# Single K tiles in the first two splits of weights, another order of the first loads, and other slots for the pairs' steps of attention

## The chip, the core and the metric

The kernel runs on one core of one Trainium2 chip. The metric is the device time of that core in microseconds (us): the median of the runs of a program.

## What is computed

Two layers, each with one input projection, two branches of mixing, and one output projection; 256 positions, D = 2048, float32 throughout. Cut to what matters:

```python
def hybrid_layer(x, ...):
    h = rmsnorm(x, norm_g)
    c_a, c_glu, c_gate, q_down, kv_down, k_pe, m_gate, g_conv, g_mla = split(h @ w_in)
    # branch A: convolution
    u = c_a * sigmoid(c_glu)
    u = causal_depthwise_conv(u, conv_w, width=31) + conv_b
    y_conv = (silu(layernorm(u)) * silu(c_gate)) @ w_proj_conv
    # branch B: 16 heads, query and key of 192 (128 plain, 64 rotary), value of 128
    q = rmsnorm_per_head(rmsnorm(q_down) @ w_uq)            # then rope on 64 of 192
    k_nope, v = split(rmsnorm(kv_down) @ w_ukv)
    k = rmsnorm_per_head(concat(k_nope, k_pe))              # then rope on 64 of 192
    o = softmax(q @ k.T * 192**-0.5, mask: key chunk <= query chunk, chunks of 64) @ v
    y_mla = (o * silu(m_gate)) @ w_proj_mla
    y = sigmoid(g_conv) * y_conv + sigmoid(g_mla) * y_mla
    return x + y @ w_out
```

## The kernel before

**Products.** Every float32 product is made of three products of TensorE's F32R type. A matrix is split into `hi` (a cast to F32R) and `lo` (what the cast left); the three are hi·hi, hi·lo and lo·hi. Weights come as *pieces* of two K tiles (`KS` = 2; a K tile is 128 rows, by 512 columns, or 384 for `uq`) on SP's DMA queue (`load`, four pieces ahead). `split_hi` has ScalarE cast a piece three ahead, `split_lo` has VectorE subtract it two ahead, and `product` runs a *block* (a weight matrix by up to 512 columns): for each piece twelve matmuls, six for each half `t` of the positions, in the order that `order_of_products` gives. Only piece 0 is loaded and split by single K tiles. A block's accumulators are evacuated one slot after its last piece; blocks take turns on two sets of accumulators.

**The order of work.** `order_of_layer` writes it out: a `glu` block (8 pieces), the three `down` blocks, two more `glu`, and then for each of the 8 pairs of heads `uq` (2 pieces), `ukv` (2 pieces), and a `glu` or `cgate` block (8 pieces): a period of 12 pieces, about 35 us. Then the gates and the projections follow.

**Slots.** After each piece `background` counts a clock on by one and issues whatever is due: first the steps that `at_slot` entered for this slot or an earlier one, then, as far as a budget of VectorE's time lasts, the next entries of `fill` (the taps of the depthwise convolution, one by one), and, by a budget of ScalarE's, a tap scaled ahead (`assist`): VectorE then adds it with one instruction (an *added* tap) in place of two (*direct* taps). `InOrder` chains the instructions of each engine, so that an engine's order in the program is the order in which the steps were called. As it also issues them, every instruction in the profile stands at its line, L127.

**A pair's steps.** `attention(b)` enters them all once the pair's `ukv` block is issued, at slots counted from there: `stats` (norm factors of q and k), `scale_k` (scales k by its factor and parks q and k in DRAM through GpSimd's queue, `turn_d`), `back_in("qk")` (fetches them transposed in 32-blocks), `blockwise` (VectorE transposes within the blocks), `split_nope` and `split_rope` (casts on ScalarE, subtractions on VectorE one slot later), `scores` (TensorE, tile `s`), `maxima`, `exponentials` (ScalarE, tile `pr`, parked through GpSimd), `back_in("p")`, `turn_p` (transposes `pr`), `split_p` (casts and subtracts them into tile `pv`, which also holds the values), `values`, `outputs`. With a period of 12 slots and steps out to slot 34, the steps of three pairs are interleaved at any time.

**A glu block's end.** `glu_evac` has ScalarE compute the sigmoid and VectorE the product, both named `su` in the rows; the accumulators are free when VectorE has read them. The block after the next one, `ukv`, takes the same accumulators.

**The start.** ScalarE's queue loads the gains with x's first tile (`gx`), then x's tiles 1, 2–3 and 4–5; SP's loads pieces 0, 1, 2, then x's tiles 6–7, piece 3, x's 8–11, piece 4, x's 12–15. `first_h` scales a tile of x by its gain (`h_hi` on ScalarE, `h_lo` on VectorE); `split_hi` calls it ahead of the cast of the piece that needs it. `warm` is a chain of matmuls on zeros, ahead of the first product.

Of the kernel before, what the change touches and what calls it, by code (L numbers as in the profile page):

```python
# [12 lines left out]
F32 = mybir.dt.float32  # L13
F32R = mybir.dt.float32r
# [6 lines left out]
P = 128  # L21
T = 2
# [33 lines left out]
R_QA, R_KVA, R_QR, R_KR, R_N = 0, LORA, 2 * LORA, 2 * LORA + ROPE, 2 * LORA + 2 * ROPE  # L56

KS = 2
N_WARM = 8

# [1 line left out]
EVAC_AT = 1  # L64
FETCH_AT, TURNED_AT = 4, 8

STATS_AT, SCALE_AT, QK_BACK_AT, QK_TURN_AT, NOPE_AT, ROPE_AT, SCORES_AT = 2, 3, 6, 11, 12, 14, 17
MAX_AT, EXP_AT, P_BACK_AT, P_TURN_AT, P_SPLIT_AT, VALUES_AT, O_AT = 18, 19, 23, 28, 30, 32, 34

REVOLUTION_PIECES = 6  # L70

# [44 lines left out]
def trunk(ctx: ExitStack, tc: tile.TileContext, xT, x, g_in, pos, win, wuq, wukv, wpc, wpm, wo, cst, rows, invf, out):  # L116
# [19 lines left out]
    pe, vec, act, gps, sp = (InOrder(e) for e in (nc.tensor, nc.vector, nc.scalar, nc.gpsimd, nc.sync))  # L136
# [7 lines left out]
    work = pool("work", 1)  # L144
# [7 lines left out]
    tp_p = pool("tp", 2, space=PSUM)  # L152
# [30 lines left out]
    def load(i):  # L183
        if i >= len(pieces) or i in loaded:
            return
        ap, n = pieces[i]
        loaded[i] = t = raw_p.tile([P, KS, n], F32, tag="raw", name=f"raw{i}")
        for a in range(0, KS, 1 if i == 0 else KS):
            k = slice(a, a + 1 if i == 0 else KS)
            sp.dma_start(t[:, k, :], ap[:, k, :])  # L190

    def split_hi(i):
        if i >= len(pieces) or i in highs:
            return
        load(i)
        highs[i] = split_p.tile([P, KS, pieces[i][1]], F32R, tag="hi", name=f"hi{i}", bufs=4)
        for a in range(0, KS, 1 if i == 0 else KS):
            k = slice(a, a + 1 if i == 0 else KS)

            for step in ("w", "h") if i == a == 0 else ("h", "w"):  # L200
                if step == "w":
                    act.copy(highs[i][:, k], loaded[i][:, k])
                    if i == 0:
                        split_lo(0, k)
                elif i * KS < NCT:
                    for c in range(i * KS + k.start, i * KS + k.stop):
                        first_h(c)
        for a in range(1, LOAD_AHEAD + 1):
            load(i + a)

    def split_lo(i, k=slice(0, KS)):
        if i >= len(pieces) or done.get(i, (0, 0, 0))[2] >= k.stop:
            return
        lo = done[i][1] if i in done else split_p.tile([P, KS, pieces[i][1]], F32R, tag="lo", name=f"lo{i}")
        vec.tensor_sub(lo[:, k], loaded[i][:, k], highs[i][:, k].bitcast(F32))
        done[i] = highs[i], lo, k.stop
# [61 lines left out]
    def order_of_products(i, last):  # L278

        two = range(2)
        if i == 0:
            return [(t, kk, p) for kk in range(KS) for p in ((0, 1, 2) if kk else (0, 2, 1)) for t in range(T)]
        high, low = (lambda t, p: [(t, kk, p) for kk in range(KS)]), (lambda t: [(t, kk, 2) for kk in range(KS)])
        if last:
            return high(0, 0) + high(0, 1) + high(1, 0) + low(0) + high(1, 1) + low(1)
        return [e for t in two for p in two for e in high(t, p)] + low(0) + low(1)

    def product(planned, stat, evacuate, evac_at=EVAC_AT, costs=(0.0, 0.0), before=None):  # L290
        nk, n, mine = planned
        blocks_begun[0] += 1
        pts = [acc_p.tile([P, 512], F32, tag=f"acc{blocks_begun[0] % 2}{t}", name=f"acc{mine[0]}_{t}") for t in range(T)]

        def evac():
            for t in range(T):
                evacuate(t, pts[t][:, :n])

        for j, i in enumerate(mine):
            for a in range(HI_AHEAD + 1):  # L300
                split_hi(i + a)
                if a <= LO_AHEAD:
                    split_lo(i + a)
            hi, lo, _ = done[i]
            if before:
                before(j)
            for t, kk, part in order_of_products(i, j == len(mine) - 1):
                k = j * KS + kk
                sh, sl = stat(k, t)
                stationary, w = ((sh, hi), (sl, hi), (sh, lo))[part]  # L310
                pe.matmul(
                    pts[t][:, :n], stationary, w[:, kk, :],
                    start=k == 0 and part == 0, stop=k == nk - 1 and part == 2,
                )
            if j == len(mine) - 1:
                steps.insert(0, (clock[0] + 1 + evac_at, costs, evac))
            background(n)
# [76 lines left out]

    ident = const.tile([P, P], F32, name="ident")
    make_identity(nc, ident)
    ones = const.tile([P, P], F32, name="ones")
    vec.memset(ones, 1.0 / D)

# [11 lines left out]
    def load_x(engine, a, b):  # L411
        engine.dma_start(x_in[:, a:b, :], xT[:, a:b, :])
# [3 lines left out]
    act.dma_start(gx, g_in)  # L416
    load_x(act, 1, 2)
    act.copy(sin2[:, 0, 0, :], ones[:, :HALF])
    for i in range(3):
        load(i)  # L420
    load_x(act, 2, 4)
    load_x(act, 4, 6)
    load_x(sp, 6, 8)
    load(3)
    load_x(sp, 8, 12)
# [1 line left out]
    load_x(sp, 12, 16)  # L427


    zeros = work.tile([P, 512], F32R, tag="junk", name="zeros")  # L430
    vec.memset(zeros.bitcast(F32), 0.0)
    warm = tp_p.tile([P, 512], F32, tag="tp", name="warm")
    for i in range(N_WARM):
        pe.matmul(warm, zeros[:, :P], zeros, start=i == 0, stop=i == N_WARM - 1)

# [53 lines left out]
    def first_h(c):  # L489
        g = gx[:, c : c + 1]  # L490
        act.activation(h_hi[:, c, :], x_tile(c), AF.Copy, scale=g)
        vec.scalar_tensor_tensor(
            h_lo[:, c, :], x_tile(c), g, h_hi[:, c, :].bitcast(F32), op0=ALU.mult, op1=ALU.subtract
        )
        if c == NCT - 1:
            vec.tensor_copy(gains, gx[:, : DEPTH * NCT])
# [824 lines left out]
```

## Time and profile before

| | |
|---|---|
| median of 3 runs | 1892.09 us (1891.77 to 1892.33) |
| the profiled execution's own time | 1891.51 us |
| its span | 1889.7 us |
| TensorE matmul (PE) busy | 1881.9 us, 100% |
| TensorE weight load (PEld) busy | 1589.4 us, 84% |
| VectorE (DVE) busy | 1601.2 us, 85% |
| ScalarE (ACT) busy | 1331.5 us, 70% |
| GpSimd (POOL) busy | 392.9 us, 21% |
| TensorE's granted clock | 9 tenths or more in all 40 slices |
| DMA | 441.91 MB, mean 234 GB/s |

The page is of one execution. A row of the views below names the engine, the line, the operation, the tile it writes and those it reads, partitions x elements, how often (x); in the timeline the first two numbers are the time from the span's start and the length, and a bracket gives the idle time before it and what ended that. The chain goes back from the last instruction, at each step to what released it. The engine's name with `<-` stands for the writer of what was waited for.

### The profile page before, as it was taken

The page shows a single profiled execution, that of the slowest core. Times are in us where ns is not written, and L with a number is a line of the kernel's source. Part 1 is how long each engine was busy: PE and PEld are TensorE (multiplying, and loading weights), DVE is VectorE, ACT ScalarE, POOL GpSimd, SP SyncE. Part 2 cuts the span into 40 slices and gives each one's busy share as a digit, 9 for nine tenths or more (in the row PEclk, how much of TensorE's full clock was granted, in tenths as well). Part 3 has the DMA queues.
Part 4 walks back from the last instruction along what each step waited for, and adds up shares of the span by engine and source line. Part 5 has one row for each costly group of instructions (what it writes and reads, how often), then busy time and mean ns, then how long its engine had stood idle before and what let it go on. Part 6 is the DMA issues. An engine that isn't in the chain of part 4 may idle for free.

```text
span 1889.7 us, 27378 instructions
## 1 busy us (share of the span) xinstructions
PE 1881.9 (100%) x8744; PEld 1589.4 (84%) x8744; DVE 1601.2 (85%) x2623; ACT 1331.5 (70%) x2350; POOL 392.9 (21%) x734
## 2 busy tenths in 40 slices
PE   9999999999999999999999999999999999999999
PEld 8988888888888888888899888888888888888887
DVE  6899998899999998765679898888999999985654
ACT  7677878878787866544557688688887878474442
POOL 1043433332200000121211443343322000001200
PEclk9999999999999999999999999999999999999999
DMA  9678778776765566677866877787767555666764
GB/s 321 218 251 275 258 236 272 256 256 225 229 210 192 187 218 217 216 236 258 281 209 216 263 263 243 260 266 241 257 228 237 199 189 195 225 213 215 237 224 164
DMA packets 137232, 441.91 MB, mean 234 GB/s; under 512 B 23296, under 2 KB 27136, under 8 KB 137088
## 3 DMA queue, kind: packets, MB, share of 16 engines
q1 hardware_dynamic: 104256, 358.84, 56.5%
q0 software_dynamic: 31968, 80.26, 13.4%
q8 instruction: 68, 1.11, 0.2%
q10 hardware_dynamic: 864, 1.07, 0.2%
q14 instruction: 76, 0.62, 0.1%
HBM read 397.61 MB, written 42.47 MB: 233 GB/s over the span
## 4 chain that ended last, share of the span: by engine, by line
PE 97%; DVE 2%; ACT 1%; DMA 0%; issue 0%; POOL 0%; ACTq 0%; DVEq 0%
PE acc L127 94%; PE s L127 2%; PE o_ps L127 1%; DVE lo L127 1%; DVE v_t L127 0%; DMA x_in<-in_xT 0%; ACT hi L127 0%; ACT tap L127 0%; DVE qk L127 0%; DMA turn_d<-pr 0%; PE tp L127 0%; ACT qk L127 0%; DVE rsq_t L127 0%; DVE ym L127 0%; ACT junk L127 0%
## 5 line engine op out<-in xcount | busy, mean ns | idle before, releaser
L127 ACT CAST hi<-raw 128x1024 fp32r<-128x1024 f32 (+3 forms) x689 | 699.5, 1022 | 411.7 <-PE acc L127 351.7
L127 DVE TENSOR_TENSOR lo<-raw,hi 128x1024 fp32r<-128x1024 f32 (+3 forms) x689 | 811.4, 1181 | 207.8 <-PE acc L127 164.7
L127 PE MATMUL acc<-hi,hT 128*128 128x512 f32 (+2 forms) x1728 | 419.8, 382 | 0.0
L127 PEld LDWEIGHTS acc<-hi,hT 128*128 128x128 f32 x1728 | 319.8, 188 | 59.1
L127 ACT ACTIVATE tap<-u_t,cst 128x256 f32<-128x256 f32 x598 | 260.9, 500 | 14.6 <-DVE v_t L127 13.6
L127 PE MATMUL acc<-hi,h_hi 128*128 128x512 f32 (+2 forms) x864 | 261.3, 384 | 1.1 <-ACT hi L127 1.1
L127 PE MATMUL acc<-hi,h_lo 128*128 128x512 f32 (+2 forms) x864 | 260.1, 382 | 0.0
L127 PE MATMUL acc<-lo,h_hi 128*128 128x512 f32 (+2 forms) x864 | 229.8, 382 | 0.0
L127 PE MATMUL acc<-lo,hT 128*128 128x512 f32 (+2 forms) x864 | 229.3, 382 | 0.0
L127 DVE TENSOR_TENSOR v_t<-v_t,tap 128x512 f32<-128x512 f32 x299 | 205.3, 687 | 10.1
L127 PEld LDWEIGHTS acc<-hi,h_lo 128*128 128x128 f32 x864 | 161.2, 188 | 30.2
L127 PEld LDWEIGHTS acc<-hi,h_hi 128*128 128x128 f32 x864 | 160.4, 188 | 31.0 <-ACT hi L127 1.5
L127 PEld LDWEIGHTS acc<-lo,h_hi 128*128 128x128 f32 x864 | 160.9, 188 | 30.0
L127 PEld LDWEIGHTS acc<-lo,hT 128*128 128x128 f32 x864 | 160.6, 188 | 29.9
L127 POOL DMA_DIRECT2D turn_d<-gate x176 | 95.6, 551 | 321.5 <-DVE gate L127 278.0
L127 DVE SCALAR_TENSOR_TENSOR v_t<-u_t,cst,v_t 128x256 f32<-128x256 f32 x362 | 155.4, 480 | 3.0
L127 POOL DMA_DIRECT2D turned<-turn_d x82 | 45.9, 560 | 519.6 <-DVE v_t L127 317.3
L127 PE MATMUL acc<-hi,oT 128*128 128x512 f32 x512 | 128.1, 390 | 0.0
L127 PE MATMUL acc<-hi,yT 128*128 128x512 f32 x512 | 128.0, 389 | 0.0
L127 PE MATMUL acc<-hi,ycT 128*128 128x512 f32 x512 | 127.8, 389 | 0.0
L127 PE MATMUL acc<-hi,qkc 128*128 128x512 f32 (+1 forms) x512 | 119.0, 364 | 0.2
L127 PEld LDWEIGHTS acc<-hi,oT 128*128 128x128 f32 x512 | 96.1, 188 | 20.1
(171 smaller groups left out, 2139.8 us busy)
## 6 DMA issues: line engine op xcount, KB each, us to landing
raw<-in_win SPq DMA_DIRECT2D x383, 512.0 KB, 4.2
raw<-in_wpm SPq DMA_DIRECT2D x64, 512.0 KB, 3.2
raw<-in_wpc SPq DMA_DIRECT2D x64, 512.0 KB, 4.0
raw<-in_wo SPq DMA_DIRECT2D x64, 512.0 KB, 4.3
raw<-in_wukv SPq DMA_DIRECT2D x32, 512.0 KB, 5.2
turned<-turn_d POOLq DMA_DIRECT2D x50, 256.0 KB, 4.5
raw<-in_win SPq DMA_DIRECT2D x32, 384.0 KB, 4.4
raw<-in_wuq SPq DMA_DIRECT2D x32, 384.0 KB, 3.0
```

The lines of the kernel that those rows point to most:

```text
L127: ins = getattr(self.engine, name)(*a, **k)
```

## The change

- The warming zeros are 256 columns wide instead of 512, are set ahead of VectorE's other constants, and 17 matmuls use them instead of 8.
- Pieces 0 and 1 are both split by single K tiles: x's tile, the cast of its half of the piece, the subtraction of that half, then the same for the second. Piece 1 is still loaded by one DMA. The products of piece 1 go by K tile like those of piece 0.
- x's tiles 4–5 are loaded on SP's queue, behind piece 1 and ahead of piece 2, and no longer on ScalarE's.
- Ten of the fourteen steps of a pair stand at other slots, one or two later; the transposes of q and k, the plain split, the split of the probabilities and the values stay.

```diff
@@ -56,7 +56,7 @@
 R_QA, R_KVA, R_QR, R_KR, R_N = 0, LORA, 2 * LORA, 2 * LORA + ROPE, 2 * LORA + 2 * ROPE
 
 KS = 2
-N_WARM = 8
+N_WARM = 17
 
 
 
@@ -64,8 +64,8 @@
 EVAC_AT = 1
 FETCH_AT, TURNED_AT = 4, 8
 
-STATS_AT, SCALE_AT, QK_BACK_AT, QK_TURN_AT, NOPE_AT, ROPE_AT, SCORES_AT = 2, 3, 6, 11, 12, 14, 17
-MAX_AT, EXP_AT, P_BACK_AT, P_TURN_AT, P_SPLIT_AT, VALUES_AT, O_AT = 18, 19, 23, 28, 30, 32, 34
+STATS_AT, SCALE_AT, QK_BACK_AT, QK_TURN_AT, NOPE_AT, ROPE_AT, SCORES_AT = 3, 5, 8, 11, 12, 15, 18
+MAX_AT, EXP_AT, P_BACK_AT, P_TURN_AT, P_SPLIT_AT, VALUES_AT, O_AT = 19, 20, 24, 29, 30, 32, 35
 
 REVOLUTION_PIECES = 6
 
@@ -194,14 +194,15 @@
             return
         load(i)
         highs[i] = split_p.tile([P, KS, pieces[i][1]], F32R, tag="hi", name=f"hi{i}", bufs=4)
-        for a in range(0, KS, 1 if i == 0 else KS):
-            k = slice(a, a + 1 if i == 0 else KS)
+        singly = i < 2
+        for a in range(0, KS, 1 if singly else KS):
+            k = slice(a, a + 1 if singly else KS)
 
             for step in ("w", "h") if i == a == 0 else ("h", "w"):
                 if step == "w":
                     act.copy(highs[i][:, k], loaded[i][:, k])
-                    if i == 0:
-                        split_lo(0, k)
+                    if singly:
+                        split_lo(i, k)
                 elif i * KS < NCT:
                     for c in range(i * KS + k.start, i * KS + k.stop):
                         first_h(c)
@@ -280,8 +281,8 @@
 
 
         two = range(2)
-        if i == 0:
-            return [(t, kk, p) for kk in range(KS) for p in ((0, 1, 2) if kk else (0, 2, 1)) for t in range(T)]
+        if i < 2:
+            return [(t, kk, p) for kk in range(KS) for p in ((0, 2, 1) if i == kk == 0 else (0, 1, 2)) for t in range(T)]
         high, low = (lambda t, p: [(t, kk, p) for kk in range(KS)]), (lambda t: [(t, kk, 2) for kk in range(KS)])
         if last:
             return high(0, 0) + high(0, 1) + high(1, 0) + low(0) + high(1, 1) + low(1)
@@ -394,6 +395,8 @@
 
     ident = const.tile([P, P], F32, name="ident")
     make_identity(nc, ident)
+    zeros = work.tile([P, 256], F32R, tag="junk", name="zeros")
+    vec.memset(zeros.bitcast(F32), 0.0)
     ones = const.tile([P, P], F32, name="ones")
     vec.memset(ones, 1.0 / D)
 
@@ -416,10 +419,11 @@
     act.dma_start(gx, g_in)
     load_x(act, 1, 2)
     act.copy(sin2[:, 0, 0, :], ones[:, :HALF])
-    for i in range(3):
-        load(i)
+    load(0)
+    load(1)
     load_x(act, 2, 4)
-    load_x(act, 4, 6)
+    load_x(sp, 4, 6)
+    load(2)
     load_x(sp, 6, 8)
     load(3)
     load_x(sp, 8, 12)
@@ -427,9 +431,7 @@
     load_x(sp, 12, 16)
 
 
-    zeros = work.tile([P, 512], F32R, tag="junk", name="zeros")
-    vec.memset(zeros.bitcast(F32), 0.0)
-    warm = tp_p.tile([P, 512], F32, tag="tp", name="warm")
+    warm = tp_p.tile([P, 256], F32, tag="tp", name="warm")
     for i in range(N_WARM):
         pe.matmul(warm, zeros[:, :P], zeros, start=i == 0, stop=i == N_WARM - 1)
 
```

## The prediction

> **What bounds the kernel now.** I read the page's chain first, then TensorE's waits over the whole span, then the chain of waits of the first 12 us, then the timeline of one pair's period (258 to 299 us), engine by engine.
>
> ```profile
> span 1889.7 us, 27378 instructions
> ...
> PE 97%; DVE 2%; ACT 1%; DMA 0%; issue 0%; POOL 0%; ACTq 0%; DVEq 0%
> ```
>
> ```profile
> PE s L127 <- DVE qk_t L127: 0.7, 1, 0.7
> ```
>
> The chain is TensorE's own matmuls for 97% of the span. After the start, its waits as the view lists them come to one: 0.7 us before one pair's scores. So this change cannot shorten the work; it can only remove or add waits of TensorE, and the question is which waits. There is little to remove and no limit to what can be added. The start, from the chain of waits and from TensorE's and ScalarE's timeline:
>
> ```profile
> 1.73 6.34 DMA x_in<-in_xT
> 8.06 0.02 issue
> 8.09 0.91 ACT h_hi L127 x2
> ```
>
> ```profile
> 1.59 3.78 PE L127 MATMUL warm<-zeros 128*128 128x512 f32 x8 [1.59 <-DVE zeros L127]
> 5.17 1.19 PE L127 MATMUL acc<-hi,h_hi 128*128 128x512 f32 x2
> 6.16 0.92 PE L127 MATMUL acc<-lo,h_hi 128*128 128x512 f32 x2
> 6.92 0.62 PE L127 MATMUL acc<-hi,h_lo 128*128 128x512 f32 x2
> 7.38 0.62 PE L127 MATMUL acc<-hi,h_hi 128*128 128x512 f32 x2
> ...
> 9.98 0.50 PE L127 MATMUL acc<-hi,h_hi 128*128 128x512 f32 x1 [1.06 <-ACT hi L127]
> ```
>
> ```profile
> 4.06 0.62 ACT L127 CAST hi<-raw 128x512 fp32r<-128x512 f32 x1 [0.88 <-DMA raw<-in_win]
> ```
>
> Real products start at 5.17. The second piece of weights starts at 9.98, 1.06 late: x's third and fourth tiles land at 8.06, ScalarE scales both (0.91), then casts the whole piece.
>
> **The start, part by part.** With single K tiles ScalarE scales one x tile (half of 0.91), casts half of the piece (0.62, the 128x512 row), and TensorE can go on at 8.09 + 0.45 + 0.62, about 9.2 instead of 9.98: **-0.8 us**. At most the whole wait goes (-1.1); at worst nothing, if x's third tile lands later. It then does not wait at the third piece: two scalings and two half casts more bring that piece's cast to an end near 11.8, and twelve products of 0.23 (0.46 for two, from 6.92 to 7.38) from 9.2 end at 11.9. x's fifth and sixth tiles move from ScalarE's queue to SP's, behind the second piece and ahead of the third. All the same bytes are due by then, so the third piece lands at most as much later as they land earlier, and its cast isn't reached before 10.8; I cost the move at nothing, covered by those casts, and at half a microsecond if the cover is gone. SP's later loads keep their order. The zeros come first on VectorE and are half as long, so the warming products start some 0.4 earlier and 17 of 256 columns take about as long as 8 of 512. The first real product does not start earlier by it: it needs the scaled first tile.
>
> In the rows two products take 0.99 at 5.17 and 0.46 from 6.92 on. The Trainium skill, "TensorE: Matmul & The Clock Gate", Part 1, puts such a step down to a gate that opens after a busy window of about 3.4 us which runs free of the kernel's start; by it the step may come earlier or later than here in any run, and would take a part of the gain at random. The rows agree as far as one profile can; the sum does not use it.
>
> **The pairs' slots.** A pair's steps are issued after given pieces of weights; a period is 12 pieces (8 glu or gate, 2 uq, 2 ukv). In the order that the new slots give, scores follow the rope subtractions as before, but no longer right behind the factors and the k scaling on VectorE: these now stand a piece earlier and a piece later. So the 0.7 wait before scores goes: **-0.7 us**. What comes instead is read at the end of the period, where ukv's first product needs the accumulator of the glu block, which is free when VectorE's `su` has read it:
>
> ```profile
> 285.10 0.95 DVE L127 TENSOR_TENSOR pv<-pr,pv 128x768 fp32r<-128x768 f32 x1
> 285.96 1.82 DVE L127 TENSOR_TENSOR lo<-raw,hi 128x768 fp32r<-128x768 f32 x2
> 287.70 1.41 DVE L127 TENSOR_TENSOR v_t<-v_t,tap 128x512 f32<-128x512 f32 x2
> 290.54 1.23 DVE L127 TENSOR_TENSOR lo<-raw,hi 128x1024 fp32r<-128x1024 f32 x1 [1.42 <-ACT hi L127]
> 293.28 0.87 DVE L127 SCALAR_TENSOR_TENSOR su<-acc,rinv_x,su 128x256 f32<-128x256 f32 x2 [1.52 <-ACT su L127]
> 294.07 1.21 DVE L127 TENSOR_TENSOR lo<-raw,hi 128x1024 fp32r<-128x1024 f32 x1
> 295.20 1.67 DVE L127 SCALAR_TENSOR_TENSOR v_t<-u_t,cst,v_t 128x256 f32<-128x256 f32 x4
> 296.79 1.22 DVE L127 TENSOR_TENSOR lo<-raw,hi 128x1024 fp32r<-128x1024 f32 x1
> 297.92 1.83 DVE L127 STREAM_TRANSPOSE qk<-qk 128x768 f32<-128x768 f32 x2
> ```
>
> ```profile
> 286.11 1.28 ACT L127 ACT_TABLE_LOAD   x1 [3.18 <-DVE pv L127]
> ...
> 289.46 1.99 ACT L127 CAST hi<-raw 128x1024 fp32r<-128x1024 f32 x2
> 291.48 1.28 ACT L127 ACT_TABLE_LOAD   x1
> 292.77 0.84 ACT L127 ACTIVATE su<-acc,rinv_x 128x256 f32<-128x256 f32 x2
> ```
>
> ```profile
> 293.38 0.51 PE L127 MATMUL acc<-lo,qkc 128*128 128x384 f32 x2
> 293.91 0.94 PE L127 MATMUL acc<-hi,qkc 128*128 128x512 f32 x3
> ```
>
> ```profile
> 363.53 0.51 PE L127 MATMUL acc<-lo,qkc 128*128 128x384 f32 x2
> 363.88 0.63 PE L127 MATMUL acc<-hi,qkc 128*128 128x512 f32 x2
> ```
>
> The reader is to see a ring. VectorE ends the split of the pair's probabilities (`pv`), ScalarE waits for it 3.18 us, loads the exponentials' table, computes them, casts two pieces (1.99), loads the sigmoid's table, computes `su`; VectorE waits for that, and TensorE starts ukv 0.53 after the uq pair where an unhindered start is 0.35 after it (the last block's rows): 0.18 late. After `su` VectorE works without a gap to the transposes, and the ring closes through ScalarE:
>
> ```profile
> 264.65 0.72 ACT L127 ACTIVATE qk<-qk,gqk 128x512 f32<-128x512 f32 x1 [0.45 <-DVE qk L127]
> ```
>
> ```profile
> 269.95 0.42 DVE L127 TENSOR_TENSOR pv<-acc,pv 128x256 fp32r<-128x256 f32 x1 [0.36 <-ACT junk L127]
> ```
>
> ScalarE waits 0.45 for the transposes, runs on through the k split and ukv's eviction, and VectorE waits 0.36 for that; nothing in the ring waits for TensorE. So whatever is added to the ring is added to every period, and TensorE follows it once its slack is used up.
>
> What the new slots add, with the exponentials a piece later and the factors too:
> - a pair of direct taps now stands between the two pieces ahead of the factors, where no step was due any more: half of the four in 1.67, **+0.84**;
> - the split of one 384-wide piece now stands ahead of the maxima: half of 1.82, **+0.91**;
> - behind `su`, one added tap (half of 1.41) and two direct ones replace four direct ones (1.67): 0.70 + 0.84 - 1.67 = **-0.13**;
> - between exponentials and sigmoid one cast instead of two: half of 1.99, **-1.00**.
>
> That is +0.62 a period. The scaling of k stands later but within the same stretch, and adds nothing there. It does move what follows it: parking and fetching q and k. GpSimd's order now has the fetch of q and k behind the parking of the previous pair's probabilities, which waits for the exponentials:
>
> ```profile
> 289.86 2.20 POOL L127 DMA_DIRECT2D turn_d<-pr  x4 [3.88 <-ACT pr L127]
> ```
>
> ```profile
> qk<-turn_d POOLq DMA_DIRECT2D x32, 384.0 KB, 5.4
> ...
> pr<-turn_d POOLq DMA_DIRECT2D x16, 384.0 KB, 4.5
> ```
>
> Exponentials 1.62 later (0.84 + 0.91 - 0.13) put that parking at 291.5 to 293.7, and the first fetch lands 4.5 (the same size, for `pr`) to 5.4 later, at 298.2 to 299.1. VectorE reaches the transposes at 297.92 + 0.62 - 0.13 = 298.4. So it waits 0 to 0.7 for data that were long there before; the second fetch is issued 0.55 behind, the second transpose comes 0.9 behind, so the first decides. I take the middle, **+0.4**: 1.0 a period, with 0.6 and 1.3 as ends, and 1.7 if the second of two fetches in a row comes late.
>
> There are 8 pairs a layer. The first ring that is lengthened ends at the fourth ukv block, the last at the eighth: 5 periods. The eighth block starts with slack; its accumulator is half free by about 363:
>
> ```profile
> 362.27 1.27 ACT L127 ACTIVATE gate<-acc,rinv_x 128x512 f32<-128x512 f32 x2
> ```
>
> that is 0.9 to 0.6 before 363.88, some 0.8. A layer loses 5 x 1.0 - 0.8 = 4.2, two layers **+8.4** (with 0.6: 4.4; with 1.3: 11.4; with 1.7: 15.4).
>
> **The sum.** -0.8 - 0.7 + 8.4 = +6.9 on the profiled execution's own 1891.5, 0.6 under the median of the three runs shown. On the median that is 1892.1 + 6.9 = **1899.0**. Everything else of the change costs nothing that I can find: the outputs' copy, scores and the last transposes keep pieces of cover, and the other steps move with their pair.
>
> **Rivals.** A change of 0.2%, 3.8 us, is about what a measurement of this kernel can tell from none.
>
> *The ring does not bind (not slower).* Place: VectorE between the first added tap pair and the maxima. If VectorE there waits for TensorE to give buffers back (each split of weights needs the buffer of three pieces before), the taps and the split fill gaps and are free, while the dropped cast's 1.00 remains. Then the late starts (0.18 here, similar in a few blocks) go as well: -0.8 - 0.7 - 0.7 = -2.2, 1889.9. It decides where less than 0.4 of the 1.75 reaches the maxima. Against it: the view shows no gap of VectorE in that stretch but the 0.36; for it: the stretch as changed isn't traced. Chance 0.20.
>
> *The fetch is free.* VectorE never waits for q and k; the ring grows by 0.62 alone: 4.4 - 1.5 = +2.9, 1895.0, still within 0.2%. It decides where the fetch lands within 4.7 us. For it: the `pr` fetches of the same size at 4.5. Against it: the 5.4. Chance 0.18. The Trainium skill, "DMA: Bandwidth & Descriptors", section on the SWDGE path, fits such a transfer as 2.0 us plus bytes over 436 GB/s, an estimate of 2.9 us for 384 KB; by that page this rival is the outcome. The trace does not agree: 5.4 at the median of 32.
>
> *Faster by over 0.2%.* It would need more than all waits named here. Chance 0.04. That the steps don't move is no rival: the order follows from the constants.
>
> **How the numbers follow.** The forecast (the ring binds and the fetch costs something) has 0.58 and alone gives slower by over 0.2%; its own range is 1896 to 1906. The first two rivals, 0.38 together, lie within 0.2%. The range takes both in and leaves the tails: 1889.5 to 1906. Slower 0.58, same 0.38, faster 0.04.
>
> **What would show it.** At the start: the wait of 1.06 down to 0.2 to 0.4. Scores without a wait. Ukv's first product 1 to 2 us behind uq's last in the fifth to seventh block of each layer, released by `su` or `gate`; VectorE waiting for the fetch ahead of `qk<-qk`; a single cast between exponentials and sigmoid. The forecast is wrong if ukv starts on time, or if the loss stands elsewhere: at scores, or at a split of weights that comes too late.

## The result, and the profile after

The changed kernel takes 1911.9 us (median of 5, 1910.95 to 1915.6) beside 1892.33 of the kernel before: a ratio of 1.0108, 95% interval 1.0094 to 1.0123, some 20 us slower. The forecast was slower, by 7, with 1906.0 as its upper end. The sign and the place were right, the size was a third of the measured one.

The page's first line and its chain, then the waits of TensorE (us in total, times, longest):

```profile
span 1909.0 us, 27347 instructions
...
PE 89%; DVE 5%; issue 3%; ACT 2%; DMA 1%; POOL 0%; ACTq 0%; DVEq 0%
```

```profile
PE acc L127 <- DVE su L127: 8.3, 5, 2.4
PE acc L127 <- ACT gate L127: 5.5, 4, 2.0
PE acc L127 <- DVE lo L127: 1.6, 3, 0.7
...
PE s L127 <- DVE qk_t L127: 0.5, 2, 0.2
PE acc L127 <- ACT hi L127: 0.4, 1, 0.4
```

The chain is no longer TensorE's alone. TensorE now waits at most `ukv` blocks for `su` or `gate` to free the accumulators: read from start to start, the first products of twelve of the sixteen `ukv` blocks come 16.2 us late together, against 1.0 before. One of them, 1.53 behind the last `uq` pair where an unhindered start is 0.35 behind it:

```profile
296.36 0.51 PE L127 MATMUL acc<-lo,qkc 128*128 128x384 f32 x2
297.89 0.93 PE L127 MATMUL acc<-hi,qkc 128*128 128x512 f32 x3 [1.01 <-DVE su L127]
```

The wait at the start is down from 1.06 to 0.4, and the waits at scores are short.

One ring of a `glu` block after the change, VectorE and then ScalarE:

```profile
261.32 0.88 DVE L127 SCALAR_TENSOR_TENSOR su<-acc,rinv_x,su 128x256 f32<-128x256 f32 x2 [3.67 <-ACT su L127]
...
266.04 1.84 DVE L127 STREAM_TRANSPOSE qk<-qk 128x768 f32<-128x768 f32 x2
...
274.69 0.88 DVE L127 SCALAR_TENSOR_TENSOR v_t<-u_t,cst,v_t 128x256 f32<-128x256 f32 x2
...
288.19 0.95 DVE L127 TENSOR_TENSOR lo<-raw,hi 128x768 fp32r<-128x768 f32 x1
...
290.81 0.16 DVE L127 TENSOR_TENSOR nb<-nb,rs_p 128x4 f32<-128x4 f32 x1
...
297.26 0.87 DVE L127 SCALAR_TENSOR_TENSOR su<-acc,rinv_x,su 128x256 f32<-128x256 f32 x2 [3.32 <-ACT su L127]
```

```profile
291.04 1.28 ACT L127 ACT_TABLE_LOAD   x1 [2.04 <-issue]
...
294.39 1.05 ACT L127 CAST hi<-raw 128x1024 fp32r<-128x1024 f32 x1
295.46 1.28 ACT L127 ACT_TABLE_LOAD   x1
296.75 0.84 ACT L127 ACTIVATE su<-acc,rinv_x 128x256 f32<-128x256 f32 x2
```

The tap pair (274.69) and the 384-wide split (288.19) stand ahead of the maxima, and a single cast lies between the tables, as forecast. The ring takes 297.26 - 261.32 = 35.94 us where TensorE's own work of a period takes 34.7 (the shortest pitch of the `ukv` blocks in such a period, 34.69). Both kernels have two added taps and two pairs of direct ones in each such period: no tap is new. One was moved out of the time in which VectorE waits for the exponentials and `su`.

A `cgate` block, GpSimd and then VectorE:

```profile
330.57 2.17 POOL L127 DMA_DIRECT2D turn_d<-pr  x4 [4.09 <-ACT pr L127]
332.74 1.12 POOL L127 DMA_DIRECT2D qk<-turn_d  x2
```

```profile
334.76 1.23 DVE L127 TENSOR_TENSOR lo<-raw,hi 128x1024 fp32r<-128x1024 f32 x1 [0.70 <-ACT hi L127]
338.60 0.98 DVE L127 STREAM_TRANSPOSE qk<-qk 128x768 f32<-128x768 f32 x1 [2.61 <-DMA qk<-turn_d]
```

The fetch is issued behind the parking, as forecast, and VectorE waits 2.61 for it, not 0 to 0.7. In the `glu` ring above the transposes waited 0.07. That is the difference between the two kinds of block: with `su` to do, VectorE reaches the transposes 7.4 after the exponentials end, without it 5.7.

### The profile page after: what moved, and what is told of

It reads as the page before. It is cut to its first block, busy times and chain, and to the rows that moved or that the text cites. A ratio compares the mean times of both kernels' runs of the same rounds, so it can differ in the third digit from the quotient of the medians.

```text
span 1909.0 us, 27347 instructions
## 1 busy us (share of the span) xinstructions
PE 1886.5 (99%) x8753; PEld 1590.6 (83%) x8753; DVE 1601.1 (84%) x2627; ACT 1324.2 (69%) x2345; POOL 392.3 (21%) x734
## 4 chain that ended last, share of the span: by engine, by line
PE 89%; DVE 5%; issue 3%; ACT 2%; DMA 1%; POOL 0%; ACTq 0%; DVEq 0%
PE acc L127 87%; DVE lo L127 2%; PE s L127 1%; DVE v_t L127 1%; PE o_ps L127 1%; ACT hi L127 1%; DMA qk<-turn_d 1%; ACT L127 1%; DVE qk_t L127 1%; POOL turn_d L127 0%; ACT pr L127 0%; DVE qk L127 0%; DMA x_in<-in_xT 0%; ACT tap L127 0%; DVE rsq_t L127 0%
## 5 line engine op out<-in xcount | busy, mean ns | idle before, releaser
L127 POOL DMA_DIRECT2D turn_d<-qk x128 | 69.9, 554 | 242.0 <-DVE qk L127 167.6
```

The source lines that it names most:

```text
L127: ins = getattr(self.engine, name)(*a, **k)
```

## The experiments

"Period" below is the time from one pair's first exponential to the next one's, read from the traces: before, 35.1 to 36.0 in `glu` (35.1 in the ring that the prediction read) and 34.2 to 34.4 in `cgate` blocks; after, 35.8 to 37.4. A layer's last period, behind which no `ukv` block stands, is left out below. "Above" and "below" the kernel before is against its median in the same set of runs, 1891.2 to 1891.7.

**The fetch ahead again.** `QK_BACK_AT`: 8 → 7.

> The changed kernel with one slot put back: q's and k's fetch at 7 in place of 8, so that GpSimd has it ahead of the previous pair's parking of probabilities again. Fetch theory (the loss is a chain exponentials, parking, fetch, transposes, maxima, exponentials, 36.2 to 38.0 us from transposes to transposes in the trace of after): no wait ahead of the transposes, only the longer work of VectorE stays, 1893 to 1899 us. Work theory (taps and split ahead of the maxima make the loss, the wait only fills slack): 1907 or more.

1900.45 us, ratio 1.0044 (1.0032 to 1.0057). No first transpose waits from the third pair on, and the middle periods of a layer are 35.8 to 36.4 in both kinds of block. So of the 20 us some 11 are the fetch's place; the other 9 are neither theory's figure: more than the forecast's ring, less than the work theory wants.

```profile
PE acc L127 <- DVE su L127: 5.8, 5, 2.1
PE acc L127 <- ACT gate L127: 3.1, 4, 0.9
```

**The start alone.** All slots as before.

> The changed kernel with all slots as before: only the start is changed. Both theories: the first wait for the cast shrinks as in the trace of after, where products ran 0.76 ahead of before from 12 us on; 0.5 to 0.9 below before, about 1891.5 us, within what the measurement can tell from none.

1890.65 us, ratio 0.9995 (0.9986 to 1.0003), 0.7 less in the medians. The wait for the second piece's casts is gone from TensorE's list; the kernels with the old start show 1.1, 1.4 and 1.8 there, those with the new one 0 to 1.0.

**The slots alone.** The kernel before with the new slots.

> The kernel before with all the new slots and its own start. Both theories: the loss of after and 0.8 more, 1911 to 1915 us. If it came out well below 1910, the loss would hang on the start too.

1910.68 us, ratio 1.0103 (1.0089 to 1.0117), just under the lower end. That is 19.3 above the kernel before; with the 0.7 of the start off it is 18.6, where the whole change costs 19.6. The slots are the loss, and start and slots add within 1 us, about what such medians can tell.

**The fetch behind, alone.** Before with `QK_BACK_AT`: 6 → 8.

> The kernel before with one slot moved: q's and k's fetch at 8 in place of 6, so that GpSimd has it behind the previous pair's parking of probabilities; no step of VectorE, ScalarE or TensorE moves. Fetch theory: in the gate blocks, where VectorE reaches the transposes 5.8 to 6.9 after the exponentials and parking and fetch take 2.6 and 5.8, about 1.5 of waiting for each of three blocks a layer, 1894 to 1899 us. Work theory: nothing, 1892.

1893.83 us, ratio 1.0013 (1.0004 to 1.0022), just under the range. VectorE waits where it was expected, and TensorE's slack covers most:

```profile
DVE qk L127 <- DMA qk<-turn_d: 8.5, 8, 2.2
```

Moving the fetch behind the parking costs 2.5 here and 11 in the changed kernel, where the exponentials stand a piece later: what it costs is set by the ring it is in.

**Exponentials later, factors not.** `STATS_AT, SCALE_AT, QK_BACK_AT`: 3, 5, 8 → 2, 3, 6.

> The changed kernel with factors (2), scaling (3) and fetch (6) back at their old slots; rope, scores, maxima, exponentials and what follows stay at the new ones. VectorE's order then has no tap pair ahead of the factors and two direct taps instead of an added and two direct ones behind su. Ring theory: against before a 384-wide split more (0.89), two direct taps fewer (0.84) and one cast fewer on ScalarE (1.00), so the ring falls from 35.1 to about 34.2, under TensorE's 34.8, ukv starts on time and scores do not wait: 1888.5 to 1890.5 us. Rival (the later exponentials themselves cost, by the piece they stand later): 1894 or more.

1888.82 us, ratio 0.9984 (0.9976 to 0.9993): faster than both kernels. It is 2.9 below the kernel before, of which 0.7 is the start. Period 34.3 to 35.0; TensorE's list has only this of `su` and splits:

```profile
PE acc L127 <- DVE su L127: 0.7, 2, 0.5
...
PE acc L127 <- DVE lo L127: 0.2, 1, 0.2
```

Later exponentials cost nothing by themselves; with one cast between the tables they even gain.

**Factors later, exponentials not.** `STATS_AT, SCALE_AT`: 3, 5; the fetch at 6, the rest as before.

> The changed kernel with only factors (3) and scaling (5) later, the fetch (6) and all from rope on at their old slots. VectorE's ring gets an added tap more (0.70), ScalarE keeps two casts between exponentials and sigmoid. Ring theory: 35.1 + 0.7 = 35.8 a period, like the 35.79 of the run with the fetch ahead: 1898 to 1902 us. Rival (the later exponentials cost): little over before, 1891 to 1894.

1901.77 us, ratio 1.0056 (1.0043 to 1.007); period 35.8 to 36.9 in `glu` blocks. By this run it is the later factors and what they move, not the exponentials; that it is the tap, moved into the ring, is what the next run tests.

**The taps put off.** On top of the fetch at 7:

```diff
+            at_slot(STATS_AT - 1, lambda: None, 1.0)
             at_slot(STATS_AT, stats, 2.2)
```

> The changed kernel with the fetch at 7 and one more step per pair that does nothing but charge 1.0 us of VectorE's budget in the slot ahead of the factors, so that the scheduler puts two direct taps of each period off to a later part of the layer. All taps are still done. Ring theory: 35.79 less 0.84 is 34.95, TensorE hardly waits: 1890 to 1893.5 us, 8 below the run with the fetch at 7 alone. Rival (the place of the steps and not the taps): 1899 to 1901 as there.

1899.4 us, ratio 1.0039 (1.0027 to 1.0052): the total missed the ring theory's range by 6. Among the pairs it did what was expected: ukv is late in three blocks only, by 0.3 each. So it is the taps. Those put off came back in layer 0: the last one ends 12 us later than before, and the projection of the convolution finds its operand missing twice. From the last `ukv` block of layer 0 to the first of layer 1 it takes 709.7 us, against 699.3 in the run with later exponentials; that is nearly all of the 10.6 between the two.

```profile
PE acc L127 <- ACT ycT L127: 5.6, 2, 3.2
```

**The fetch behind in the faster kernel.** `QK_BACK_AT`: 6 → 8 there.

> As the run with factors at 2 and scaling at 3, but the fetch at 8, behind the parking of probabilities. Work of VectorE and ScalarE is the same. Fetch chain: transposes to maxima 24.6 less 0.84, and 2.1 (exponentials), 3.9 (parking) and 5.8 (fetch) more, 35.5 to 36 us a period where gate blocks are, hidden in the glu blocks: 1892 to 1898 us, 2 to 8 above its twin. If it costs nothing, the parking is no part of a ring when VectorE has slack.

1904.67 us, ratio 1.0072 (1.006 to 1.0085), 15.9 above its twin, twice the upper end. VectorE has slack, and it doesn't help, for the chain through GpSimd closes on itself. VectorE and GpSimd:

```profile
336.19 0.98 DVE L127 STREAM_TRANSPOSE qk<-qk 128x768 f32<-128x768 f32 x1 [4.56 <-DMA turn_d<-gate]
```

```profile
326.20 2.17 POOL L127 DMA_DIRECT2D turn_d<-pr  x4 [9.87 <-ACT pr L127]
328.37 1.13 POOL L127 DMA_DIRECT2D qk<-turn_d  x2
```

By its links: 4.6 from the first exponential to the fetch's issue, 5.2 to 7.7 until it lands, 24.7 from the transposes to the end of the maxima, 1.4 to the exponentials: 35.9 to 38.4, and the periods read 36.4 to 38.5 in `cgate` blocks. The sum had taken 5.8 for the landing and a shorter way to the maxima. (The row names a parking's DMA as releaser; the fetch landed 0.1 before the transpose.)

**The parking from ScalarE's queue.** `park` of `pr` issued by `act` instead of `gps`, all slots as changed.

> The changed kernel with all its slots; only the parking of the probabilities is issued from ScalarE's queue, right behind the exponentials, so that the fetch of q and k at slot 8 has no parking ahead of it on GpSimd. Fetch theory (what costs is GpSimd waiting for the exponentials): as the run with the fetch at 7, 1898 to 1903 us, the upper end if the four issues cost ScalarE 0.1 each or more. Rival (slot 8 is too late in itself, whoever parks): 1907 or more.

1930.42 us, ratio 1.0208 (1.0193 to 1.0223): missed by both. The first transposes never wait, as the fetch theory has it, but the four issues hold ScalarE 2.06 inside the ring:

```profile
298.82 2.06 ACTq L127 DMA_DIRECT2D turn_d<-pr  x4
300.93 1.04 ACT L127 CAST hi<-raw 128x1024 fp32r<-128x1024 f32 x1 [2.14 <-PE acc L127]
```

35.8 + 2.06 = 37.9; the period reads 37.3 to 39.0. I had allowed 0.1 an issue, though GpSimd's rows showed 0.55.

**Work added to the ring.** The faster kernel with the last maximum taken twice, then three times (`for _ in range(2)`, `range(3)`).

> The faster kernel (factors 2, scaling 3, fetch 6, the rest new) with one more maximum of 0.70 us per pair on VectorE, inside the ring; the output is the same. Ring theory: about 34.2 + 0.7 = 34.9 against TensorE's 34.7, at most 0.2 for each of six periods a layer: 0 to 3 above its twin's 1888.8. If VectorE's work counts as such: 16 x 0.70 = 11.2 above. If VectorE is off the path: nothing.

> The same with two more maxima per pair, 1.40 us. Ring theory: 35.6 against 34.7, 0.9 for each of six periods a layer less 1 to 2 of slack: 7 to 11 above 1888.8, not twice the run with one. If VectorE's work counts as such: 22.4 above. If VectorE is off the path: nothing.

1894.0 us, ratio 1.0014 (1.0005 to 1.0024), and 1901.45, ratio 1.0055 (1.004 to 1.007): 5.2 and 12.6 above their twin, both some 2 over the range (the kernel before took 0.5 less beside them than beside the twin). Periods 35.0 to 35.7 and 35.7 to 36.6. The second 0.70 costs 7.4 over 12 periods, 0.62 each; the first costs less. It is a threshold, TensorE's 34.7, crossed a little earlier than taken.

**Made waits.** 48 of them, in the kernel before.

> The kernel before with 48 made waits of TensorE in the gates' and projections' blocks, each a small product of zeros, a chain of 3 to 13 copies on ScalarE, and another small product. Asked: after which length of wait TensorE's products take 0.43 us in place of 0.23, and for how long. The traces so far have it after waits of 2.2 and 2.5 us but not after others of 1.9 to 2.5. If the length alone decides, there is a threshold; if it is the place of the wait in a fixed window, the share rises with the length. The whole is slower by the waits, some 100 to 150 us.

One run, 2091.71 us. Two of the waits:

```profile
1978.77 0.33 PE L127 MATMUL idle_c<-idle_b 128*128 128x128 f32 x1 [1.74 <-ACT idle_b L127]
1978.93 3.13 PE L127 MATMUL acc<-hi,yT 128*128 128x512 f32 x8
```

```profile
970.48 0.33 PE L127 MATMUL idle_c<-idle_b 128*128 128x128 f32 x1 [1.67 <-ACT idle_b L127]
970.64 2.07 PE L127 MATMUL acc<-hi,yT 128*128 128x512 f32 x8
```

From start to start these are 2.06 and 1.89 long; eight products after them take 3.13 and 2.07. Of the 12 waits up to 1.95 none is followed by slow products; of the 36 from 2.06 to 5.66, 27 are, by 5 to 12 products of 0.43 in place of 0.23, a loss of 1.2 to 2.7 us, mostly 1.6. So the length alone does not decide above 2 us.

The place does. In this trace TensorE's granted clock changes only at points of a grid of 3.41 us, and each slow stretch is one window of that grid; three last two. The wait of 2.06 above lies whole in one window; one of 2.61 (from 1763.31) that cost nothing is split between two. In these rows the first two numbers are the window and its length, then TensorE's busy time; the last three are the granted clock, the DMA's share and its GB/s:

```profile
1976.20:1979.62 3.42, 1.46 (x7) 0.95 (x6) 2.18 (x3) 1.93 (x6) 0.00 (x0) 1.00 0.55 188
1979.62:1983.03 3.41, 3.41 (x9) 2.65 (x9) 0.00 (x0) 0.92 (x1) 0.00 (x0) 0.50 0.36 138
1761.16:1764.58 3.42, 2.37 (x12) 1.76 (x10) 3.26 (x7) 1.89 (x5) 0.00 (x0) 1.00 0.42 143
1764.58:1767.99 3.41, 2.08 (x10) 1.73 (x11) 2.16 (x3) 1.19 (x4) 0.55 (x1) 1.00 0.49 162
1767.99:1771.40 3.41, 3.41 (x17) 2.82 (x16) 2.25 (x3) 3.20 (x4) 0.00 (x0) 1.00 0.30 118
```

Counted by the starts of the products, 37 windows at full clock in all the traces of this case hold 2.14 us or more of idle TensorE, and each is followed by a window at half the clock; no window with 2.10 or less is.

## Why the prediction was wrong

- **The start, -0.8:** right (-0.7 in the medians, products 0.76 ahead in the changed trace).
- **The wait before scores, -0.7:** the long one went; three of 0.3 to 0.4, start to start, took its place.
- **The ring's growth, +0.62:** right as a growth, 35.8 against 35.1. Wrong was the step to TensorE, "5 x 1.0 - 0.8". The ring has to be set against TensorE's 34.7, not against its own old length: it was above that in `glu` blocks already and recovered in `cgate` blocks (34.4), which the sum read as a ring without slack that merely keeps pace. At 35.8 there is no block left to recover in: 1.1 for each of six periods a layer, where the case without a fetch wait had 0.62 for five less 0.8. That case was put at 1895.0; the run with the fetch at 7 gives 1900.45. The pitches from the third `ukv` block of a layer to the eighth, both layers added, bear this out: they exceed 34.7 a period by 3.4 before, by 12.6 with the fetch at 7, and by 0.1 in the run with exponentials later and factors not.
- **The fetch, +0.4 a period, 4 in all:** the step that failed most; it measures 11. Some 6 of these stand in the pitches just named (18.7 over after the change), some 3 behind the eighth block, which the sum left out. The wait was worked out from one `glu` block and used for all: in the changed trace the first transposes wait 2.6 to 3.4 in `cgate` blocks. And I priced it as a pause in VectorE's ring, when it closes a second ring: exponentials, parking, fetch, transposes, maxima. In the `cgate` blocks, without `su`, VectorE is early, and that second ring sets the period.
- **The rivals:** "the ring does not bind" fell: 0.70 of work added to the ring costs 0.62 a period once it is over TensorE's. "The fetch is free" fell too; the estimate of 2.9 us for 384 KB from the fit in the Trainium skill, "DMA: Bandwidth & Descriptors", section on the SWDGE path, is not met in any run: these fetches took 3.3 to 8.6.
- **Not in the sum:** the half-speed products. One late start of the changed trace, by 2.6, was followed by them:

```profile
1173.24 3.38 PE L127 MATMUL acc<-hi,qkc 128*128 128x512 f32 x8 [2.43 <-DVE su L127]
```

Eight products take 3.38 where the made wait of 1.89 left 2.07, some 1.6 us lost with their successors. Another of the same length (ending at 225.99) went without: two windows of the 3.41 us grid hold 1.3 and 1.2 of it, where one window holds all of this one.

What makes a fetch land sooner in one block than in another was not taken apart. In the changed trace the first of two takes 4.5 to 5.9 in `glu` and 5.7 to 6.4 in `cgate` blocks, where GpSimd issues eight parkings of 64 KB right behind it in place of eight of 32 KB; whether these slow it was not tried.

## What to carry to other kernels

Where steps of one iteration feed the next through in-order engines, list every closed chain, the queues of DMA issues among them, and compare each one's length with the bound engine's period, block kind by block kind; the largest excess, times the periods, is about the loss. Moving a step by one slot moves fill work too: what matters is whether that work lands in the ring or in the shadow of a wait. A DMA issue that sits behind a wait in its engine's queue inherits that wait.

## What was not expected of the hardware

TensorE loses more than the wait when over 2.1 us of idle time fall in one window of 3.41: its granted clock is half in the next window, which costs another 1.2 to 2.7 us. The same idle time spread over two windows costs nothing more. The Trainium skill, "TensorE: Matmul & The Clock Gate", Part 1, has the clock fall after an idle window of about 3.4 us that runs free of the kernel. The traces agree on the window and its fixed grid, but it need not be wholly idle: 2.14 of 3.41 us sufficed. And four strided DMA issues of 96 KB each held ScalarE 2.06 us, GpSimd 2.17.
